# FFN up product by blocks, seven products for eight, on a normalised input, with weight sums added by DMA into the raw tiles

## The chip, the cores and the metric

The kernel runs on one core of one Trainium2 chip. The time is the device time of one execution in microseconds (us); lower is better. The engines are TensorE (PE; its weight loads are listed as PEld), VectorE (DVE), ScalarE (ACT), GpSimd (POOL) and SyncE (SP, which here only issues DMAs). DMA transfers are issued by SP, ACT or POOL and run on 16 shared DMA engines.

## What is computed

One layer of a hybrid encoder block on x of 512 tokens x 1024 channels, all in float32: an RMS norm, a joint input projection, gated linear attention (GLA) and forgetting attention (FoX) side by side, a gated merge, an output projection, and then the FFN that the change is about. Cut to that part:

```python
x = x + y @ w_out                                            # (512, 1024)
a, val = jnp.split(rmsnorm(x, norm_ffn_g) @ w_up, 2, axis=-1)    # w_up: 1024 x 5632
a = causal_dwconv(a, conv_w, conv_b)                         # width 3, over tokens
return rmsnorm(x + (jax.nn.gelu(a) * val) @ w_down, norm_final_g)   # w_down: 2816 x 1024
```

RMS norm divides each token by its root mean square, so the division can be done before or after the product with w_up.

## The kernel before

Features lie on the 128 partitions and tokens on the free axis. D = 1024 channels are KD = 8 blocks of 128; the FFN width of 2816 is NF = 22 feature tiles of 128, for `a` and for `val` each.

**A product in three matmuls.** To keep float32 accuracy, each operand is split into a high part (a cast to float32r) and a low part (what is left). `mm3` multiplies high by high, high by low and low by high: three matmuls, each up to 512 columns wide, with a stationary operand of 128 x 128.

**Weights as pieces.** All weights come through one list of pieces of 128 x 1024 floats (512 KB), numbered in the order of use. A piece is loaded from DRAM into a `raw` tile by SP, cast to `wh` by ScalarE and its residual `wl` is made by VectorE (`split_next`). `piece()` hands out the next piece and first splits up to NW = 3 pieces ahead; `wh` and `wl` have three buffers, `raw` has two (NRAW), and in the down product two more (NRAWX). Pieces 8 to 23 are the token products, 24 to 35 the gates used within the FoX attention, 36 to 51 the other gates and the branches, 52 to 59 w_out, then w_up and w_down.

**Order of the work.** The order in which instructions are written in the code is a priority. A scheduler places them on each engine in that order, but takes a later one when an earlier one isn't ready by its estimate; each engine then runs its own list strictly in order. In the attention, `fill` mixes gate products among the heads by a hand-written pattern, and `load_cb` brings the forget-gate rows `cb` of a head from DRAM (`nct`) one head ahead, with a POOL addition after each.

**From w_out to the FFN.** For each of eight channel blocks, w_out's product gives the new x (`xr`); ScalarE and VectorE make its scaled high and low parts `x2h`, `x2l` (not yet divided by the root mean square), POOL sums squares into `ssum`, and TensorE transposes `xr` into `x2t` for the final residual. The first feature tile of the up product follows; then `rms_of_sum` forms the per-token factor `rb` (ones matmul, a reciprocal root on VectorE, a broadcast by an identity matmul, a copy on ScalarE).

**Up product.** For each f of 22, two `feature_tile` calls (`pa` for `a`, `pv` for `val`) of 8 x 3 matmuls of 512 columns. VectorE multiplies `pa` by `rb` into `ap` with two columns of zeros in front; the convolution is an Identity with scale and bias on ScalarE and two taps on VectorE, then a Gelu on ScalarE, a POOL product with `rb`, and a VectorE product with `pv` into `act`. Meanwhile VectorE forms the sums of activations that the down product needs, and POOL issues eight DMAs that build four sums of blocks of w_down in DRAM (`wsum`).

**Down product.** It is already done by blocks, with seven products of half-size blocks for eight (`product`, p = 0 to 6): 512 columns per matmul, with one piece used up in 12 matmuls. Its last product runs 256 columns at a time for half of the tokens, then the final norm and the stores follow.

Of the kernel before, what the change touches and what calls it, by code (L numbers as in the profile page):

```python
# [18 lines left out]
P = 128  # L19
# [31 lines left out]
NW = 3  # L51


@with_exitstack
def hybrid_kernel(ctx: ExitStack, tc, xT, wp, wd, wf, pp, aw2, qkg, fing, out):
# [21 lines left out]
    def pmm():  # L77
        return bank("mm")
# [12 lines left out]
    down_blocks = [wd[0], wsum[0], wsum[1], wd[2], wsum[2], wd[3], wsum[3]]  # L91
    ND = KD + wp.shape[0]
    NP = ND + NPB * len(down_blocks)

    def width(n):
        return 512 if n >= ND and (n - ND) % NPB == NPB - 1 else 1024

    raws, splits, taken, first_copy = [], [], [0], []
    spare = {}

    def load_raw():
        n = len(raws)
        if n < KD:
            raws.append(slabs[n])
            nc.sync.dma_start(slabs[n], wf[n])
            return
        if n >= ND + NRAW + NRAWX and (n - ND) % (NRAW + NRAWX) >= NRAW:
            raw = xpool.tile([P, 1024], F32, tag="xc", name="raw", bufs=NRAWX)
        else:
            raw = wpool.tile([P, 1024], F32, tag="raw", name="raw", bufs=NRAW)  # L110
        if n < ND:
            nc.sync.dma_start(raw, wp[n - KD])
        else:
            c, m = (n - ND) % NPB * 1024, width(n)
            nc.sync.dma_start(raw[:, :m], down_blocks[(n - ND) // NPB][:, c : c + m])
        raws.append(raw)

    def split_next():
        n = len(splits)
        raw = raws[n]  # L120
# [12 lines left out]
        else:  # L133
            m = width(n)
            nc.scalar.copy(out=hi[:, :m], in_=raw[:, :m])  # L135
            nc.vector.tensor_sub(out=lo[:, :m], in0=raw[:, :m], in1=hi[:, :m].bitcast(F32))  # L136
        splits.append((hi, lo))

    def piece():
        n = taken[0]  # L140
        taken[0] += 1
        while len(splits) < min(NP, n + NW + sum(i in spare for i in range(n + NW))):
            if len(raws) == len(splits):
                load_raw()
            split_next()
            while len(raws) < min(NP, len(splits) + NRAW + (NRAWX if len(raws) >= ND + NRAW else 0)):
                load_raw()
# [62 lines left out]
    cpool.tile([P, 56], F32, name="padc")  # L210
# [43 lines left out]
    def fill(n=1 << 30):  # L254
# [9 lines left out]
    xab = [xpool.tile([P, (KD - NRAWX) * T], F32R, name=f"x{c}") for c in "hl"]  # L264
    xc = [xpool.tile([P, 1024], F32R, tag="xc", name=f"xc{i}", bufs=NRAWX) for i in range(NRAWX)]
    xh, xl = (
        [xab[i][:, k * T : (k + 1) * T] for k in range(KD - NRAWX)] + [c[:, i * T : (i + 1) * T] for c in xc]
# [868 lines left out]
```

## Time and profile before

| | |
|---|---|
| runs, us | 730.02, 730.12, 731.63 (median 730.12) |
| profiled execution, us | 731.21 |
| its span, first to last instruction, us | 729.5 |
| granted TensorE clock | 0.997 |
| DMA moved, MB | 108.78 (mean 149 GB/s) |

The profile is of one execution. Its time is 1.7 us longer than its span and 1.1 us above the median of the runs. Every row names an engine, a line of the code (L136 is line 136), the tile written and the tiles read, shapes and counts; the idle time of an engine before a group and what ended it stand behind the bar. Matmuls are pipelined, so the duration of one is longer than the spacing from one to the next. Lines 151 to 153 are the three matmuls of `mm3`, whatever product calls it; lines 135 and 136 are the cast and the residual of a weight piece.

### The profile page before, as it was taken

The page shows a single profiled execution, that of the slowest core. Times are in us where ns is not written, and L with a number is a line of the kernel's source. Part 1 is how long each engine was busy: PE and PEld are TensorE (multiplying, and loading weights), DVE is VectorE, ACT ScalarE, POOL GpSimd, SP SyncE. Part 2 cuts the span into 40 slices and gives each one's busy share as a digit, 9 for nine tenths or more (in the row PEclk, how much of TensorE's full clock was granted, in tenths as well). Part 3 has the DMA queues.
Part 4 walks back from the last instruction along what each step waited for, and adds up shares of the span by engine and source line. Part 5 has one row for each costly group of instructions (what it writes and reads, how often), then busy time and mean ns, then how long its engine had stood idle before and what let it go on. Part 6 is the DMA issues. An engine that isn't in the chain of part 4 may idle for free.

```text
span 729.5 us, 9416 instructions
## 1 busy us (share of the span) xinstructions
PE 718.7 (99%) x3466; PEld 591.5 (81%) x3466; DVE 473.4 (65%) x751; ACT 351.2 (48%) x578; POOL 154.1 (21%) x162
## 2 busy tenths in 40 slices
PE   8999999999999999999999999999999999999996
PEld 5887788888888888888788888888888888788885
DVE  7774586677766766565435655555636566887876
ACT  6484324588877733234424333323322334555654
POOL 6224234323320301111221111011111011000113
PEclk9999999999999999999999999999999999999998
DMA  8153112324432242333323957788886734476653
GB/s 289 51 149 126 59 61 84 116 97 129 101 134 76 78 139 87 97 106 116 131 87 116 336 193 240 255 209 204 199 224 166 193 117 135 153 217 193 188 183 129
DMA packets 33982, 108.78 MB, mean 149 GB/s; under 512 B 3704, under 2 KB 6920, under 8 KB 33936
## 3 DMA queue, kind: packets, MB, share of 16 engines
q1 hardware_dynamic: 27552, 81.38, 34.7%
q0 software_dynamic: 4224, 23.07, 12.9%
q10 hardware_dynamic: 2160, 3.74, 1.5%
q8 instruction: 27, 0.44, 0.2%
q14 instruction: 19, 0.16, 0.1%
HBM read 106.05 MB, written 25.18 MB: 180 GB/s over the span
## 4 chain that ended last, share of the span: by engine, by line
PE 89%; DVE 3%; issue 3%; DMA 2%; ACT 1%; POOL 1%; ACTq 0%; SPq 0%; DVEq 0%; POOLq 0%
PE ps_mm L151 26%; PE ps_mm L152 25%; PE ps_mm L153 25%; PE ps_ax L152 2%; PE ps_ax L153 2%; PE ps_ax L151 2%; DVE wl L136 1%; PE ps_pt L687 1%; ACT wh L135 1%; DMA raw<-wsum 1%; DMA raw<-in_wd_dram 1%; PE ps_po L711 1%; PE ps_ax L825 1%; DMA qf<-in_wf_dram 1%; PE ps_lg L661 1%
## 5 line engine op out<-in xcount | busy, mean ns | idle before, releaser
L135 ACT CAST wh<-raw 128x1024 fp32r<-128x1024 f32 x134 | 137.7, 1029 | 221.6 <-PE ps_mm L152 116.3
L136 DVE TENSOR_TENSOR wl<-raw,wh 128x1024 fp32r<-128x1024 f32 x134 | 176.4, 1318 | 57.9 <-ACT wh L135 57.3
L151 PE MATMUL ps_mm<-xh,wh 128*128 128x512 f32 x408 | 159.9, 393 | 0.9 <-DVE wh L130 0.9
L153 PE MATMUL ps_mm<-xh,wl 128*128 128x512 f32 x408 | 159.1, 390 | 0.8 <-DVE wl L131 0.8
L152 PE MATMUL ps_mm<-xl,wh 128*128 128x512 f32 x408 | 158.9, 390 | 0.0
L153 PEld LDWEIGHTS ps_mm<-xh,wl 128*128 128x128 f32 x408 | 76.5, 188 | 17.5 <-DVE wl L131 1.4
L151 PEld LDWEIGHTS ps_mm<-xh,wh 128*128 128x128 f32 x408 | 76.6, 188 | 17.1 <-ACT xh L315 1.7
L152 PEld LDWEIGHTS ps_mm<-xl,wh 128*128 128x128 f32 x408 | 76.7, 188 | 15.1
L886 POOL TENSOR_TENSOR t<-t,rb 128x512 f32<-128x512 f32 x22 | 29.3, 1333 | 204.9 <-ACT t L885 204.9
L151 PE MATMUL ps_mm<-wh,xh 128*128 128x512 f32 x162 | 64.0, 396 | 0.0
L152 PE MATMUL ps_mm<-wl,xh 128*128 128x512 f32 x162 | 63.2, 390 | 0.0
L153 PE MATMUL ps_mm<-wh,xl 128*128 128x512 f32 x162 | 63.2, 390 | 0.0
L151 PE MATMUL ps_mm<-xc,wh 128*128 128x512 f32 x136 | 53.2, 391 | 0.0
L152 PE MATMUL ps_mm<-xc,wh 128*128 128x512 f32 x136 | 53.1, 391 | 0.0
L153 PE MATMUL ps_mm<-xc,wl 128*128 128x512 f32 x136 | 53.0, 390 | 0.0
L892 DVE TENSOR_TENSOR act<-ps_mm,t 128x512 f32<-128x512 f32 x22 | 15.2, 692 | 41.3 <-POOL t L886 41.3
L151 PEld LDWEIGHTS ps_mm<-wh,xh 128*128 128x128 f32 x162 | 30.4, 188 | 7.4 <-issue 0.7
L153 PEld LDWEIGHTS ps_mm<-wh,xl 128*128 128x128 f32 x162 | 30.4, 188 | 6.4
L152 PEld LDWEIGHTS ps_mm<-wl,xh 128*128 128x128 f32 x162 | 30.4, 188 | 6.3 <-DVE wl L136 0.2
L413 POOL TENSOR_TENSOR cb<-cb,negm 128x128 f32<-128x128 f32 x32 | 19.2, 606 | 77.0 <-DMA cb<-nct 71.4
L881 DVE SCALAR_TENSOR_TENSOR t<-ap,ppt,t 128x512 f32<-128x512 f32 x44 | 32.7, 749 | 0.7
L968 POOL TENSOR_TENSOR x2t<-x2t,fgt 128x512 f32<-128x512 f32 (+1 forms) x9 | 12.2, 1358 | 93.9 <-ACT t L959 90.4
(316 smaller groups left out, 1299.3 us busy)
## 6 DMA issues: line engine op xcount, KB each, us to landing
raw<-in_wp_dram SPq DMA_DIRECT2D x96, 512.0 KB, 3.3
wsum<-in_wd_dram POOLq DMA_DIRECT2D x6, 2816.0 KB, 14.7
raw<-wsum SPq DMA_DIRECT2D x20, 512.0 KB, 4.0
raw<-in_wd_dram SPq DMA_DIRECT2D x15, 512.0 KB, 3.6
wsum<-wsum POOLq DMA_DIRECT2D x2, 2816.0 KB, 20.9
xr<-in_xT_dram SPq DMA_DIRECT2D x8, 256.0 KB, 4.3
cb<-nct SPq DMA_DIRECT2D x8, 256.0 KB, 6.9
xr<-in_xT_dram ACTq DMA_DIRECT2D x8, 256.0 KB, 3.4
```

Source lines behind the costliest of these rows:

```text
L135: nc.scalar.copy(out=hi[:, :m], in_=raw[:, :m])
L136: nc.vector.tensor_sub(out=lo[:, :m], in0=raw[:, :m], in1=hi[:, :m].bitcast(F32))
L151: mm(ps, lhsT=ah, rhs=bh, start=start, stop=False, **k)
L152: mm(ps, lhsT=ah, rhs=bl, start=False, stop=False, **k)
L153: mm(ps, lhsT=al, rhs=bh, start=False, stop=stop, **k)
L413: nc.gpsimd.tensor_add(out=cb[:, o + n - P : o + n], in0=cb[:, o + n - P : o + n], in1=negm)
L661: mm(lg[:, :n], lhsT=qt0[:, q], rhs=kt[:, :n], start=True, stop=False)
L687: nc.tensor.transpose(pt[:, c], pr[:, c], ident)
L881: nc.vector.scalar_tensor_tensor(out=t0, in0=ap[:, w : w + T], scalar=col(C_CW + w * NF + f), in1=t0, op0=ALU.mult, op1=ALU.add)
L886: scaled = nc.gpsimd.tensor_mul(out=t0, in0=t0, in1=rb)
L892: nc.vector.tensor_mul(out=act[j][:, :, k], in0=pv.rearrange("p (i t) -> p i t", t=H), in1=t0.rearrange("p (i t) -> p i t", t=H))
L968: nc.gpsimd.tensor_mul(out=x3, in0=x3, in1=fgt[:, c])
```

## The change

Two of the 22 features keep the plain form (NCL = 2). For the other 20, taken two at a time (NSS = 10 steps), the up product is done by blocks: the 1024 channels are halved, the 512 tokens are halved, and `a` and `val` are the two halves of the output. Eight block products are replaced by seven (numbers 1 to 7) on sums of blocks of x and of w_up, Winograd's form of Strassen's method.

- The sums need one x for all, so x is normalised first: `xs`, kept as float32, is multiplied by `rb` on VectorE; four sums and seven operands' high and low parts follow (`split_x`, `minus_sum`). The POOL product with `rb` after the Gelu goes, except for the two plain features.
- A product uses one piece in 24 matmuls of 256 columns (`up_product`). The order of the products of neighbouring steps is interleaved by `SLOT`: 2, 3, 6, the next step's 1, 7, the next step's 5, 4.
- The weights' sums are not stored. A raw tile is loaded with a block, and another block is added to it by a DMA that POOL issues with an add: product 5 is loaded and added to at once; products 6, 4 and 7 add to the tile of 5, 6 and 3 after that has been split (`recipes`, `follows`). Four loads and four adds of 512 KB are made per step.
- The results are combined in PSUM and on VectorE and ScalarE: product 6 adds onto product 1's result through a sum `u`, copied back into its bank, onto which 7 and then 4 accumulate.
- The eight DMAs for the sums of w_down move from the up product to the splits of pieces 24, 27, 30, 33, 38, 42, 46 and 50, each behind a small POOL copy (`tick`).
- The transposed x goes to DRAM (`x2d`) by way of a tile `st`, and is read back by a POOL DMA after the up product. `s1` and `s2` take the places of activations no longer needed.
- The plain pairs run side by side over k, and `rms_of_sum` runs inside the first of them.

The diff, cut to its core:

```diff
+SLOT = {1: -3, 5: -1, 2: 1, 3: 2, 6: 3, 7: 5, 4: 7}
+SUM_AT = (24, 27, 30, 33, 38, 42, 46, 50)
...
+    steps = sorted((7 * g + at, g, p) for g in range(NSS) for p, at in SLOT.items())
...
+        new, before, place = {
+            1: ((u11,), None, "raw"), 2: ((u21,), None, "raw"), 3: ((u22,), None, "raw"), 5: ((u12, u11), None, "rawx"),
+            6: ((u22,), 5, "rawx"), 4: ((u21,), 6, "rawx"), 7: ((u12,), 3, "raw"),
+        }[p]
...
+    def load_raw(n):
+        new, before, m, place = recipes[n]
+        if before is not None:
+            raws[n] = raws[before]
+            return
...
+        nc.sync.dma_start(raws[n][:, :m], new[0])
+        for w in new[1:]:
+            nc.gpsimd.dma_start(raws[n][:, :m], w, accum_op=ALU.add)
+
+    def load_ahead(n):
+
+        for i in range(n, min(NP, n + 6)):
+            new, before, _, place = recipes[i]
+            if place == "rawx":
+                ahead = 6 if rawx_pool and i < ND else NRAW + NRAWX if rawx_pool else 0
+            else:
+                ahead = NRAW if i < ND - 7 * NSS else 3 if i < ND else NRAW + NRAWX
+            if i not in raws and i < n + ahead and (before is None or before in raws):
+                load_raw(i)
...
         splits.append((hi, lo))
+        if n in follows:
+            nc.gpsimd.dma_start(raw, recipes[follows[n]][0][0], accum_op=ALU.add)
+        if n in sums_at:
+            i, b, op = sums_at[n]
+            now = nc.gpsimd.tensor_copy(out=tick, in_=lo[:, 0:1].bitcast(F32))
+            with tc.issue_after(now.ins):
+                nc.gpsimd.dma_start(wsum[i], b, accum_op=op, max_dma_last_dim=KB * 512)
...
-        nc.any.tensor_copy(
-            out=x2t[:, :, c * P : (c + 1) * P], in_=pt.rearrange("p (t c) -> p t c", c=P)
-        )
+        st = bpool.tile([P, NT, P], F32, tag="st", name="st", bufs=2)
+        nc.scalar.copy(out=st, in_=pt.rearrange("p (t c) -> p t c", c=P))
+        nc.scalar.dma_start(x2d[:, :, c * P : (c + 1) * P], st)
+        nc.scalar.activation(out=xs[:, c], in_=xr, func=AF.Copy, scale=col(C_FFN + c))
...
+    plain.append((pmm(), pmm()))
+    up = (piece(), piece())
+    plain_products(plain[0], up, range(2))
+    rms_of_sum(ssum, rt, rb, cpool, "r1", between=lambda: plain_products(plain[0], up, range(2, 6)))
+    plain_products(plain[0], up, range(6, KD))
...
+    def split_x(p, src):
+        nc.scalar.copy(out=xops[p][0], in_=src)
+        nc.vector.tensor_sub(out=xops[p][1], in0=src, in1=xops[p][0].bitcast(F32))
+
+    def minus_sum(out, a, b):
+        nc.vector.scalar_tensor_tensor(out=out, in0=a, scalar=-1.0, in1=b, op0=ALU.mult, op1=ALU.subtract)
+
+    for k in range(KD):
+        nc.vector.tensor_mul(out=xs[:, k], in0=xs[:, k], in1=rb)
+    split_x(1, x11)
+    nc.vector.tensor_sub(out=x3, in0=x11, in1=x21)
+    nc.vector.tensor_sub(out=x21, in0=x22, in1=x21)
+    split_x(5, x21)
+    plain.append((pmm(), pmm()))
+    up = (piece(), piece())
+    plain_products(plain[1], up, range(KD))
+    split_x(2, x12)
+    minus_sum(x11, x21, x11)
+    minus_sum(x12, x12, x11)
+    split_x(3, x12)
+    split_x(6, x11)
+    split_x(7, x3)
+    split_x(4, x22)
...
+    def up_product(ps, p, first):
+
+        wh, wl = piece()
+        ah, al = xops[p]
+        for i in range(2):
+            for k in range(KH):
+                c = slice((i * KH + k) * P, (i * KH + k + 1) * P)
+
+                mm3(
+                    ps[:, i * H : (i + 1) * H], wh[:, c], wl[:, c], ah[:, k], al[:, k], first and i == k == 0,
+                    k == KH - 1, skip_group_check=True,
+                )
...
+    for g, p in steps:
...
+        up_product(ps, p, first)
+        if p == 1 or p == 5:
+            st[p] = joint()
+            nc.scalar.copy(out=st[p], in_=ps)
+        elif p == 6:
+            u = joint()
+            nc.vector.tensor_add(out=u, in0=ps, in1=st[1])
+            nc.scalar.copy(out=ps, in_=u)
+            minus_sum(ap[:, :, 2 : H + 2], halves(st["z"]), halves(u))
+        elif p == 7:
+            minus_sum(ap[:, :, H + 2 : T + 2], halves(ps), halves(st[5]))
+            t0 = st["t0"] = npool.tile([P, 2, T], F32, tag="t0", name="t0")
+            for i in range(2):
+                convolve(f + i, i, t0)
+        elif p == 4:
...
+                    nc.vector.tensor_mul(
+                        out=act[j][:, i, k], in0=halves(c)[:, fs], in1=t0[:, fs, i * H : (i + 1) * H]
+                    )
+            for j, k, _ in parts:
+                sums_of_acts(j, k)
...
+    nc.gpsimd.dma_start(x2t, x2d)
+    nc.gpsimd.dma_start(fgt, fing.broadcast_to([P, D]))
```

207 lines of the change are left out of this document (119 added, 88 removed).

## The prediction

> **What bounds the kernel now.** I read the page's busy table and chain first, then TensorE in order of time around the FFN up product, then stage windows, DMA and groups by line.
>
> ```profile
> PE 718.7 (99%) x3466; PEld 591.5 (81%) x3466; DVE 473.4 (65%) x751; ACT 351.2 (48%) x578; POOL 154.1 (21%) x162
> ...
> PE 89%; DVE 3%; issue 3%; DMA 2%; ACT 1%; POOL 1%; ACTq 0%; SPq 0%; DVEq 0%; POOLq 0%
> ```
>
> TensorE is busy 99% of the span and carries 89% of the chain. A matmul less is worth its spacing, as long as what feeds it keeps pace. TensorE in order of time gives two spacings; the second comes from the last product, whose tail is computed 256 columns at a time.
>
> ```profile
> 374.27 0.39 PE L151 MATMUL ps_mm<-xh,wh 128*128 128x512 f32 x1
> ...
> 596.34 0.39 PE L151 MATMUL ps_mm<-xh,wh 128*128 128x512 f32 x1
> ...
> 616.74 0.39 PE L151 MATMUL ps_mm<-wh,acth 128*128 128x512 f32 x1
> ...
> 717.00 0.28 PE L153 MATMUL ps_ax<-wh,actl 128*128 128x256 f32 x1
> ...
> 723.00 0.28 PE L152 MATMUL ps_mm<-ws,acth 128*128 128x256 f32 x1
> ```
>
> The up product runs from 374.27 to 616.74, 242.5 us. Its last 90 spacings (596.34 to 616.74) are 0.2267 us each; 50 spacings at 256 columns (717.00 to 723.00) are 0.1200 us. The 0.39 and 0.28 are pipelined durations. Half the columns cost 53% of the time. 44 tiles x 24 = 1056 matmuls x 0.2267 = 239.4 us fill the stage, so it has almost no idle time to win; only fewer columns can win.
>
> Stage windows (columns: stretch; its length and the busy us and count of PE, PEld, DVE, ACT, POOL; clock; DMA share; GB/s):
>
> ```profile
> 640.00:700.00 60.00, 60.00 (x266) 49.68 (x265) 49.75 (x64) 36.21 (x54) 6.10 (x4) 1.00 0.66 199
> 327.00:376.00 49.00, 49.00 (x230) 39.21 (x229) 23.69 (x26) 21.37 (x32) 12.96 (x8) 1.00 0.34 116
> 172.00:176.00 4.00, 3.37 (x18) 2.63 (x16) 3.89 (x10) 3.51 (x8) 2.84 (x5) 1.00 0.39 139
> ```
>
> The down product (first row) already uses up one weight piece per 12 matmuls, 2.72 us, with VectorE at 83% and TensorE never idle. That is the nearest precedent for the changed up product. The third row, in the attention, is a place where TensorE does fall idle.
>
> **The change, part by part.** Matmuls first. Two features keep the plain form (96 matmuls). The other 20 become ten steps of seven products, each 24 matmuls of 256 columns: 1680 x 0.1200 = 201.6 us in place of 960 x 0.2267 = 217.6 us: **-16.0 us**. One eighth of the columns would be 27 us; the rest is lost to the dearer short matmul. The Trainium skill, TensorE: Matmul & The Clock Gate, section Back-to-back issue gap, gives N/2.4 GHz plus about 2.5 ns for an isolated gap, 109 and 216 ns; by it the estimate would be 1680 x 0.109 - 960 x 0.216 = -24 us. The rows above read 120 and 226.7 ns, so the trace disagrees with the page and decides.
>
> A product now uses up a 512 KB piece in 24 x 0.1200 = 2.88 us where a piece lasted 24 x 0.2267 = 5.44 us. So VectorE and ScalarE must be costed. Groups by line within the up product (busy, mean ns):
>
> ```profile
> L136 DVE TENSOR_TENSOR wl<-raw,wh 128x1024 fp32r<-128x1024 f32 x37 | 45.2, 1222 | 32.2 <-ACT wh L135 32.1
> L881 DVE SCALAR_TENSOR_TENSOR t<-ap,ppt,t 128x512 f32<-128x512 f32 x36 | 27.0, 749 | 0.6
> L892 DVE TENSOR_TENSOR act<-ps_mm,t 128x512 f32<-128x512 f32 x20 | 13.8, 692 | 38.0 <-POOL t L886 38.0
> L875 DVE TENSOR_TENSOR ap<-ps_mm,rb 128x512 f32<-128x512 f32 x18 | 12.4, 687 | 10.2 <-PE ps_mm L153 10.2
> L135 ACT CAST wh<-raw 128x1024 fp32r<-128x1024 f32 x37 | 38.8, 1049 | 83.4 <-DMA raw<-in_wp_dram 48.9 <-PE ps_mm L152 34.5
> L877 ACT ACTIVATE t<-ap,ppt 128x512 f32<-128x512 f32 x18 | 14.7, 816 | 8.9 <-DVE ap L875 8.9
> L885 ACT ACTIVATE t<-t 128x512 f32<-128x512 f32 x18 | 11.4, 632 | 34.1 <-DVE t L881 34.1
> L886 POOL TENSOR_TENSOR t<-t,rb 128x512 f32<-128x512 f32 x20 | 25.8, 1292 | 184.6 <-ACT t L885 184.6
> ```
>
> Steady state, per step of 7 x 2.88 = 20.2 us. VectorE: 7 weight residuals x 1.22 = 8.5; the sum u and two differences, 0.69 + 2 x 0.75; four conv taps, 3.0; two gate products, 1.4; sums of activations 1.4 (first half) or 2.2: 16.5 to 17.3 us, 82 to 86%. ScalarE: 7 casts 7.3, three copies and one split at about 0.6 (0.57 at L826, below), two Identity 1.6, two Gelu 1.3: 12.6 us, 62%. That is the down product's load (83%, 60%), so TensorE stays the bound. One loop can still bite: product 6 ends, VectorE adds u (0.69), ScalarE copies u back into the bank (about 0.6), product 7 accumulates on it; only the next step's product 1 (2.88 us) lies between. The loop takes 1.5 us with both engines free and 3.6 with a residual (1.22) and a cast (1.05) ahead of it, so it costs 0 to 0.7 us a step. I take **+1 us** in all; the upper end is a rival. The POOL product by rb goes for these 20 features; it only delayed VectorE, so that is worth nothing.
>
> The start of the stage. Rows in order of time:
>
> ```profile
> 376.34 0.57 ACT L826 COPY x2t<-ps_ax 128x512 f32<-128x512 f32 x1
> 376.58 1.78 POOL L822 TENSOR_TENSOR ssum<-ssum,sq 128x512 f32<-128x512 f32 x1 [4.24 <-ACT sq L821]
> 385.01 1.05 ACT L135 CAST wh<-raw 128x1024 fp32r<-128x1024 f32 x1 [8.10 <-PE ps_mm L152]
> 385.72 0.95 PE L241 MATMUL ps_ax<-ones,ssum 128*128 128x2 f32 x8
> 385.76 0.34 ACTq L909 DMA_DIRECT2D fgt<-in_fing_dram  x1
> 388.28 0.16 DVE L186 TENSOR_SCALAR r1w<-r1v 128x4 int32<-128x4 int32 x1
> 388.35 1.22 DVE L136 TENSOR_TENSOR wl<-raw,wh 128x1024 fp32r<-128x1024 f32 x1
> 389.49 0.16 DVE L189 TENSOR_SCALAR rt<-r1w 128x4 int32<-128x4 int32 x1
> 391.56 1.13 PE L246 MATMUL ps_ax<-ident,rt 128*128 128x128 f32 x8 [0.42 <-DVE rt L195]
> ```
>
> The norm now runs inside the first plain pair: ssum is there at 376.58 + 1.78 = 378.4; 36 matmuls of the pair (8.2 us from 374.27) with the ones product and four transposes end at about 383.7; the broadcast (1.13) and a copy (0.6) follow, so rb stands at about 385.4. That removes the 0.42 us idle (**-0.4**). The second pair now needs both its pieces at once, and the second piece's buffer comes free only when the first pair ends (the 8.10 us wait at 385.01); cast and residual, 2.3 us, against 0.7 us of matmuls and 0.45 more that do without the residual: **+0.8 us** (0 to 1.2).
>
> Then the dear part. From rb to the end of product 6 of the first step TensorE has 2.0 (rest of pair one) + 10.9 + 5 x 2.88 = 27.3 us of work. VectorE has, before that point in code order: 8 normalising products 5.5, four sums and seven operand residuals 11 x 1.22 = 13.4, six weight residuals 7.3, both conv epilogues 7.1: 33.3 us. What can wait (two operand residuals, one sum and split) is 3.8, so the wait is at least 33.3 - 3.8 - 27.3 = 2.2 us. If VectorE keeps strictly to code order, product 2's weight residual ends 30.9 us after rb, while TensorE gets there after 18.7: 12.2 us. The row at 388.35, a weight residual set inside the reciprocal-root chain, shows that gaps are filled out of order, so I take the middle, **+7 us**.
>
> DMA. The DMA view for 400 to 600 us (queues: packets, MB, share of 16 engines; issues: KB, us to landing), and last the queue row of 522 to 543.5, one add:
>
> ```profile
> q0 software_dynamic: 4224, 23.07, 47.0%
> q1 hardware_dynamic: 5253, 19.16, 27.3%
> ...
> raw<-in_wp_dram SPq DMA_DIRECT2D x36, 512.0 KB, 6.2
> wsum<-in_wd_dram POOLq DMA_DIRECT2D x6, 2816.0 KB, 14.7
> wsum<-wsum POOLq DMA_DIRECT2D x2, 2816.0 KB, 20.9
> ```
> ```profile
> q0 software_dynamic: 528, 2.88, 68.9%
> ```
> ```profile
> 522.13 1.02 POOL L890 DMA_DIRECT2D wsum<-wsum  x1
> ```
> ```profile
> raw<-in_wp_dram SPq DMA_DIRECT2D x96, 512.0 KB, 3.3
> ```
>
> A 512 KB load takes 0.273 x 200 / 36.6 = 1.5 us of all engines, an add of that size 0.689 x 21.5 x 512/2816 = 2.7. A step has four of each: 16.8 of 20.2 us, share 0.83. No add into SBUF is in the trace; it lands in 3.3 - 1.5 + 2.7 = 4.5 us on quiet engines and 6.2 - 1.5 + 2.7 = 7.4 on loaded ones. The tightest is product 7's, added to product 3's tile: between the residual of 3 and TensorE's need lie about 11 us, less issue on POOL (1.0), cast and residual (2.3): 7.7 us. Both estimates fit, so 0; beyond 7.7 each us costs ten. Behind a late add stand, on ScalarE, the cast's followers (joint copies, conv scale); on POOL, product 5's add waits for its SP load with the adds for 7 and 4 queued behind it, due later; on SP a load waits for its tile, with at most two behind it.
>
> The four-block sums of w_down move from the up product into the attention and gates, each with a small POOL copy and a 2.8 MB transfer past POOL's and SP's queues there.
>
> ```profile
> 126.30 1.05 ACT L135 CAST wh<-raw 128x1024 fp32r<-128x1024 f32 x1 [4.33 <-PE ps_mm L153]
> ...
> 198.18 1.05 ACT L135 CAST wh<-raw 128x1024 fp32r<-128x1024 f32 x1
> ```
> ```profile
> 174.36 3.38 DMA cb<-nct
> ```
> ```profile
> cb<-nct SPq DMA_DIRECT2D x6, 256.0 KB, 6.9
> ```
>
> The first four (copies, 14.7 us each in the rows above) follow the splits of pieces 24, 27, 30 and 33, whose casts, ten from the first row to the second, are at 126.3 to 198.2 us. The cb load is on the chain where TensorE fell idle (172 to 176), so copies will meet such loads; a cb load comes a head (11 us) ahead, so a delay of 3 to 6 us mostly fits: **+1 us** (0 to 4). The detour of x2 through DRAM adds a ScalarE activation (0.6) and a DMA issue (0.34) per w_out tile (24 x 0.2267 and transposes, 6.0 us), where ScalarE is at 44% (327 to 376): 0, or 7 if that cover were gone. Its reload, 2.5 MB beside the first down pieces, has 16 us: 0 (to 2).
>
> Sum: -16.0 + 1 - 0.4 + 0.8 + 7 + 1 = -6.6. The profiled execution took 731.2, giving 724.6; it lies 1.1 above the median 730.12, which would give 723.5. I say **724**.
>
> **Rivals.** *The hand-over hides.* VectorE's order falls well, only 2.2 us are lost and no loop or cb wait appears: -16.0 - 0.4 + 2.2 = -14.2: 716. For it: gaps are filled out of order; against: 33 us of work in a 27 us window.
>
> *The u loop binds.* The schedule repeats, so a bad phase costs the same each step: 0.7 us x 10 plus followers' slips, about +9 over the forecast: 733. For it: VectorE at 86%; against: the down product at 83% without idle.
>
> *The adds come late (slower).* One mechanism: product 7's add lands after 9.5 us instead of 7.7, because engines at 0.83 queue and POOL's issue (1.0 us) is held by VectorE. Price 10 x 1.8 = +18: 742; it decides against the change from about 8.4 us on. The Trainium skill, SBUF — State Buffer, section Who interferes with whom, says that DMAs issued by GpSimd can be starved of descriptor time by VectorE while those of other queues cannot; no row here isolates that.
>
> *It doesn't do what it says.* Seven products at more than 0.126 us per matmul save less than 6 us; the tail ran 50 in a row at 0.120, so this has 0.05.
>
> **Numbers.** Forecast (720 to 729) 0.42, hidden 0.15, loop 0.20, late adds 0.18, dearer matmuls 0.05. This kernel's measurement can tell about 0.3%, 2.2 us. Faster: 0.39 + 0.15 + 0.02 = 0.56; within: 0.03 + 0.08 + 0.02 + 0.01 = 0.14; slower 0.30. The range 715 to 742 leaves out half of the late adds and a little of the hidden case; the forecast's own is 720 to 729.
>
> **What would show it.** 256-column matmuls at 0.120; VectorE at 82 to 86% in the steps; a TensorE gap of about 7 us before the first step's product 2; adds landing in 4.5 to 7.4 us. ScalarE waiting on DMA in every step, or a gap before each product 7, would make me wrong.

## The result, and the profile after

The changed kernel is slower. Four runs of it gave 739.1, 741.11, 743.35 and 743.6 us (median 742.23), beside 730.54 us for the kernel before on the same chip: a ratio of 1.0152 (95% interval 1.0114 to 1.019). The forecast was 724, with 742 as the end of its range. One of the four executions without adds (a kernel below) took 868.62 us at a granted clock of 0.753, where the other three had 0.994 to 0.995, and it is left out of the medians.

The profiled execution took 743.6 us (span 741.8), 12.3 us of span more than before. It is the longest of the four; between the medians lie 11.7 us. The page of the changed kernel: the busy times, the chain by engine, and the DMA issues (count, KB, median us from issue to landing).

```profile
PE 714.4 (96%) x4186; PEld 620.2 (84%) x4186; DVE 518.7 (70%) x787; ACT 407.4 (55%) x648; POOL 166.9 (23%) x190
...
PE 61%; DMA 17%; DVE 9%; issue 6%; ACT 4%; POOL 1%; SPq 0%; ACTq 0%; POOLq 0%; DVEq 0%
...
wsum<-in_wd_dram POOLq DMA_DIRECT2D x6, 2816.0 KB, 18.4
raw<-in_wu_dram SPq DMA_DIRECT2D x30, 512.0 KB, 4.5
rawx<-in_wu_dram POOLq DMA_DIRECT2D x30, 512.0 KB, 5.8
...
raw<-in_wu_dram POOLq DMA_DIRECT2D x10, 512.0 KB, 7.2
```

TensorE's share of the chain fell from 89% to 61%, and 17% of it is now DMA, which had 2%. The last row is product 7's add: 7.2 us at the median.

Where the 12.3 us went can be read from TensorE in order of time: the first matmul of the up product, the first and the last of 48 at 256 columns in a step, and the last of product 4 in the last step.

```profile
378.96 0.39 PE L200 MATMUL ps_mm<-xh,wh 128*128 128x512 f32 x1
...
457.88 0.28 PE L200 MATMUL ps_ax<-xh,wh 128*128 128x256 f32 x1
...
463.52 0.28 PE L202 MATMUL ps_ax<-xh,wl 128*128 128x256 f32 x1
...
630.00 0.28 PE L202 MATMUL ps_mm<-xc,wl 128*128 128x256 f32 x1
```

- Up to the up product: it begins at 378.96 where it began at 374.27: +4.7. (In the profiles of the kernels below that do the same work up to there it begins between 375.5 and 378.8, so this execution stands at the late end.)
- The up product ends at 630.1. Six matmuls of the down product stand inside it (1.4 us), so it took 249.8 us, where it took 242.5: +7.3. Two products run from 457.88 to 463.52, 47 spacings of 0.120 us, as forecast, and 16.0 us were saved; so 23.3 us of new idle and slow time stand in this stage.
- From there to the end: 113.1 against 112.8: +0.3. The three add up to 12.3.

If each start on TensorE is compared with the start before it plus the plain spacing of that matmul's shape, the changed kernel loses 9.8 us in the hand-over (376 to 440 us), 9.8 in the steps (440 to 615) and 5.6 at the end (615 to 640). The kernel before loses 1.9 in the same way around its norm, so 7.9 of the hand-over are new, and the three make up the 23.3. A typical stall of the steps, in rows of POOL, of ScalarE, of VectorE and of TensorE in order of time; the last fence is one piece of the chain in the same stretch (start, us, what):

```profile
458.58 0.86 POOL L149 DMA_DIRECT2D rawx<-in_wu_dram  x1 [7.61 <-DVE wl L181]
459.12 1.21 POOL L184 DMA_DIRECT2D raw<-in_wu_dram  x1
461.14 0.86 POOL L184 DMA_DIRECT2D rawx<-in_wu_dram  x1 [0.82 <-DVE wl L181]
```
```profile
468.00 1.05 ACT L180 CAST wh<-raw 128x1024 fp32r<-128x1024 f32 x1 [6.05 <-DMA raw<-in_wu_dram]
...
470.94 0.59 ACT L1031 COPY ps_ax<-joint 128x512 f32<-128x512 f32 x1 [0.95 <-DVE joint L1030]
```
```profile
469.08 1.23 DVE L181 TENSOR_TENSOR wl<-raw,wh 128x1024 fp32r<-128x1024 f32 x1 [5.88 <-ACT wh L180]
470.22 0.69 DVE L1030 TENSOR_TENSOR joint<-ps_ax,joint 128x512 f32<-128x512 f32 x1
```
```profile
471.58 0.39 PE L200 MATMUL ps_ax<-xh,wh 128*128 128x256 f32 x1 [2.02 <-ACT ps_ax L1031]
```
```profile
459.12 8.78 DMA raw<-in_wu_dram
```

POOL issues three adds within 2.6 us: product 5's (458.58), product 7's (459.12), product 4's (461.14). Product 7's lands after 8.78 us, and product 5's, ahead of it, after 5.39. ScalarE stands 6.05 us at its cast; behind the cast come VectorE's low part, only then u (L1030) and its copy (L1031), and product 7 starts 2.02 us late. From the cast's start to that of product 7 it is 3.58 us. Product 7 was due at 471.58 - 2.02 = 469.56, so the cast had to start at 465.98: the add had 6.9 us to land.

Windows of the changed kernel (columns as in the prediction: stretch; its length and the busy us and count of PE, PEld, DVE, ACT, POOL; clock; DMA share; GB/s):

```profile
413.42:417.80 4.38, 4.32 (x19) 3.92 (x20) 4.12 (x6) 4.12 (x6) 0.00 (x0) 0.61 0.41 120
...
440.00:590.00 150.00, 145.26 (x1180) 144.44 (x1179) 108.98 (x134) 82.23 (x102) 24.16 (x28) 0.98 0.84 196
...
471.58:475.90 4.32, 4.32 (x23) 4.32 (x24) 2.41 (x3) 1.53 (x2) 0.86 (x1) 0.60 0.61 143
```

The count in the middle row is the measure used below: 150 us hold 1250 matmuls at 0.120, and here they held 1180. The first and last rows are stretches right after a stall: the granted clock is 0.61 and 0.60 (0.50 from 472.60 to 475.80, where matmuls start 0.213 us apart instead of 0.120), and a stall of 2 to 3 us costs about 1.5 us more.

### The profile page after: what moved, and what is told of

Same layout as the page of the kernel before. It is cut to its first block, busy times and chain, and to the rows that moved or that the text cites. A ratio compares the mean times of both kernels' runs of the same rounds, so it can differ in the third digit from the quotient of the medians.

```text
span 741.8 us, 11096 instructions
## 1 busy us (share of the span) xinstructions
PE 714.4 (96%) x4186; PEld 620.2 (84%) x4186; DVE 518.7 (70%) x787; ACT 407.4 (55%) x648; POOL 166.9 (23%) x190
## 4 chain that ended last, share of the span: by engine, by line
PE 61%; DMA 17%; DVE 9%; issue 6%; ACT 4%; POOL 1%; SPq 0%; ACTq 0%; POOLq 0%; DVEq 0%
PE ps_mm L200 15%; PE ps_mm L201 14%; PE ps_mm L202 14%; DMA rawx<-in_wu_dram 7%; DMA raw<-in_wu_dram 6%; DVE wl L181 4%; PE ps_ax L201 4%; PE ps_ax L200 4%; PE ps_ax L202 4%; ACT wh L180 3%; DMA raw<-in_wp_dram 2%; DVE t L970 1%; DMA cb<-nct 1%; DMA rawx<-wsum 1%; PE ps_pt L737 1%
## 5 line engine op out<-in xcount | busy, mean ns | idle before, releaser
L200 PE MATMUL ps_mm<-xh,wh 128*128 128x512 f32 (+1 forms) x288 | 102.0, 355 | 4.1 <-ACT ps_mm L1031 3.3
L202 PE MATMUL ps_mm<-xh,wl 128*128 128x512 f32 (+1 forms) x288 | 100.8, 351 | 0.0
L201 PE MATMUL ps_mm<-xl,wh 128*128 128x512 f32 (+1 forms) x288 | 100.8, 351 | 0.0
L181 DVE TENSOR_TENSOR wl<-rawx,wh 128x1024 fp32r<-128x1024 f32 (+1 forms) x48 | 57.8, 1208 | 7.3 <-ACT wh L180 7.0
L180 ACT CAST wh<-rawx 128x1024 fp32r<-128x1024 f32 (+1 forms) x48 | 49.1, 1023 | 16.5 <-DMA rawx<-in_wu_dram 9.1
L200 PE MATMUL ps_ax<-xh,wh 128*128 128x256 f32 x120 | 35.8, 299 | 5.1 <-ACT ps_ax L1031 5.1
L200 PE MATMUL ps_ax<-xo,wh 128*128 128x256 f32 x120 | 34.2, 285 | 3.1 <-ACT wh L180 3.1
L202 PE MATMUL ps_ax<-xh,wl 128*128 128x256 f32 x120 | 35.4, 297 | 0.1
L201 PE MATMUL ps_ax<-xl,wh 128*128 128x256 f32 x120 | 35.2, 293 | 0.0
L201 PE MATMUL ps_ax<-xo,wh 128*128 128x256 f32 x120 | 34.1, 284 | 0.0
L202 PE MATMUL ps_ax<-xo,wl 128*128 128x256 f32 x120 | 34.0, 283 | 0.0
```

What stands on the lines that cost most here:

```text
L200: mm(ps, lhsT=ah, rhs=bh, start=start, stop=False, **k)
L201: mm(ps, lhsT=ah, rhs=bl, start=False, stop=False, **k)
L202: mm(ps, lhsT=al, rhs=bh, start=False, stop=stop, **k)
```

## The experiments

Each group of runs had the kernel before beside it (median 730.5 to 731.3 us); the ratios are to those runs.

| kernel | median us | ratio to before, 95% interval |
|---|---|---|
| changed kernel | 742.23 | 1.0152 (1.0114 to 1.019) |
| no adds | 725.14 | 0.9916 (0.9895 to 0.9936) |
| no sums of w_down | 739.74 | 1.0113 (1.0094 to 1.0133) |
| neither | 722.27 | 0.9881 (0.9865 to 0.9897) |
| no add for product 5 | 731.34 | 1.0011 (0.9995 to 1.0026) |
| no add for product 4 | 741.18 | 1.0147 (1.0088 to 1.0205) |
| adds of 5 and 7 swapped | 746.03 | 1.0195 (1.0164 to 1.0226) |
| u ahead of product 7's split | 741.29 | 1.0141 (1.0126 to 1.0156) |
| before, with the sums moved alone | 734.17 | 1.0041 (1.0026 to 1.0056) |
| product 7 later | 732.5 | 1.002 (1.0003 to 1.0038) |
| three edits | 743.51 | 1.0178 (1.0149 to 1.0207) |
| three edits, sums earlier | 749.89 | 1.0259 (1.019 to 1.0328) |
| product 7 later, hand-over | 731.63 | 1.0015 (1.0 to 1.003) |
| product 7 later, last step | 725.88 | 0.9927 (0.9903 to 0.995) |
| both | 725.37 | 0.9915 (0.9884 to 0.9947) |
| both, u early | 724.05 | 0.9893 (0.9876 to 0.9909) |

The theory after the result: the adds into the raw tiles come late, and the moved sums cost something too. Its first rival: the loop of product 6, u and product 7 is too long by itself, for TensorE's releaser in the rows is u's copy, not a DMA.

**No adds.**

```diff
-        for w in new[1:]:
-            nc.gpsimd.dma_start(raws[n][:, :m], w, accum_op=ALU.add)
...
-        if n in follows:
-            nc.gpsimd.dma_start(raw, recipes[follows[n]][0][0], accum_op=ALU.add)
```

> Left out: all 40 DMAs that add one weight block into a raw tile; the products read the first block alone, so every matmul, cast, subtraction and the whole steady loop stay, only these DMAs and their waits go. Theory A (the adds come late): in a step the add for product 7 lands 8.6 to 8.8 us after its issue, ScalarE's cast of that tile waits about 6 us for it, and behind the cast and VectorE's low part stand u and its copy, for which product 7 waits; the same thing happens once before product 6 in the hand-over and once at the end of the up part. Without adds the TensorE idle between 376 and 640 us falls from 24 to 5 to 9 us (what is left is the ones' matmul, 0.8, and the queue of the plain epilogue, 2 to 4), half-clock stretches there go too, and the time is 724 to 728. Rival B (the loop product 6, u, product 7 is too long by itself, or VectorE is too full): the stalls of about 2 us ahead of product 7 stay in the same steps, and the time stays at 738 to 742. The idle of attention, 100 to 376 us, stays at 10 us by both.

725.14 us, as the theory said. Its window of the steps:

```profile
440.00:590.00 150.00, 150.00 (x1252) 150.00 (x1251) 115.62 (x140) 85.69 (x107) 0.00 (x0) 1.00 0.36 106
```

The steps run at the full pace of 1250, with every cast, residual and u still in them. So the loop is not too long by itself, and the adds cost about 17 us. What stayed was the hand-over, where only 1.8 us less were lost; its longest wait is now for VectorE's backlog:

```profile
414.33 0.58 PE L198 MATMUL ps_ax<-xh,wl 128*128 128x256 f32 x1 [2.33 <-DVE wl L179]
```

**No sums, and neither.** Left out are the eight DMAs of w_down's sums.

```diff
-    down_blocks = [b11, wsum[0], wsum[1], b21, wsum[2], b22, wsum[3]]
+    down_blocks = [b11, b12, b22, b21, b22, b22, b21]
...
-        if n in sums_at:
-            i, b, op = sums_at[n]
-            now = nc.gpsimd.tensor_copy(out=tick, in_=lo[:, 0:1].bitcast(F32))
-            with tc.issue_after(now.ins):
-                nc.gpsimd.dma_start(wsum[i], b, accum_op=op, max_dma_last_dim=KB * 512)
```

> Left out: the eight DMAs that form the sums of w_down in DRAM, with the one-column copies on POOL that time them; the down part reads plain blocks of w_down instead. Theory C (the move of the sums into attention costs): TensorE's idle of 100 to 376 us falls from 10.5 to about 4.3, which is what the kernel before had there, and the time from 742 to 735 to 737; the idle of 376 to 640 stays near 24. Rival (the same idle comes from the x2 detour or from the new order of the loads): 740 to 742.

> Left out: both the 40 adds into raw tiles and the eight sums. If adds and sums have separate costs in separate places, theories A and C together, the idle is that of the kernel before plus the hand-over's 3 to 6 us, and the time is 718 to 722. If one cost only gives way to another (the steps wait for something else as soon as the adds are gone), 730 or more.

739.74 and 722.27 us; 735 to 737 was expected of the first, and 722 was the end of the range of the second. The idle of attention, gates and w_out went as expected, and the up product began 5.7 us earlier (at 373.28), but the time fell by only 2.5, because the adds' stalls fell at other steps and were larger there. Where no adds disturb, leaving out the sums gave 2.9 us (725.14 to 722.27). So costs of adds and sums lie in separate places, and the sums' is 2.5 to 2.9 us.

**The kernel before, with the sums moved alone.** The same lines, in the kernel before:

```diff
-    sum_steps = {2 * i: (i, b, ALU.bypass) for i, b in enumerate((b12, b22, b22, b21))}
-    sum_steps.update({8: (0, b11, ALU.add), 10: (2, b12, ALU.add), 12: (1, wsum[0], ALU.add), 15: (3, wsum[1], ALU.add)})
...
+        if n in sums_at:
+            i, b, op = sums_at[n]
+            now = nc.gpsimd.tensor_copy(out=tick, in_=lo[:, 0:1].bitcast(F32))
+            with tc.issue_after(now.ins):
+                nc.gpsimd.dma_start(wsum[i], b, accum_op=op, max_dma_last_dim=KB * 512)
```

> Nothing left out. The kernel before with one part of the change alone: the eight DMAs that form the sums of w_down, moved from the up part to splits 24 to 50, in attention, the gates and w_out. The prediction gave this +1 us, 0 to 4; leaving the sums out of the changed kernel gave 2.5 and 3.7 us back. If their cost is that of their place, the time is 733 to 735 with 3 to 6 us more idle on TensorE between 100 and 376 us and none elsewhere; if the place is free and only the adds' neighbourhood made them cost, 729 to 731.

734.17 us: +3.3 (the 3.7 in the expectation is the 2.9 above). The stretch 240 to 340 us (gates and w_out), first in the kernel before, then with the sums moved:

```profile
240.00:340.00 100.00, 100.00 (x446) 82.49 (x445) 65.25 (x65) 38.89 (x51) 16.87 (x13) 1.00 0.33 106
```
```profile
240.00:340.00 100.00, 98.52 (x432) 80.22 (x432) 56.58 (x63) 37.07 (x50) 22.89 (x21) 1.00 0.86 213
```

The sums raise the DMA share there from 0.33 to 0.86, and 432 matmuls stand where 446 stood: 14 x 0.2267 = 3.2 us, the whole cost. Before, the same DMAs ran inside the up product without idle.

**One add fewer: product 5's, or product 4's.** The same traffic is cut at two places of POOL's queue.

```diff
# no add for product 5
-        for w in new[1:]:
-            nc.gpsimd.dma_start(raws[n][:, :m], w, accum_op=ALU.add)
# no add for product 4
-        if n in follows:
+        if n in follows and recipes[n][1] is None:
```

> Order of the changed kernel. Left out: only the add into product 5's tile (10 DMAs of 40), which in a stalled step is issued about half a microsecond ahead of product 7's add in the same POOL queue; all else stays. If product 7's add is late because another add stands right ahead of it, its median landing falls from 7.2 us towards the 4.5 to 5 of a lone load, the casts no longer wait, and of the 9 to 10 us of TensorE idle in the steps (440 to 615 us) 3 or less stay: 731 to 735. If it is late because the DMA engines are loaded as a whole (82 to 90% busy), a quarter less adding gives a part of that, the same as the next kernel: 735 to 739.

> The other half of the pair. Left out: only the add into product 4's tile (10 DMAs of 40), which is issued about 2 us after product 7's add. The traffic cut is the same as in the kernel without product 5's add. If the place in the queue decides, product 7's add still takes 7 us and more and the idle of the steps stays at 6 to 10 us: 738 to 742. If the load as a whole decides, the same as the other: 735 to 739.

731.34 and 741.18 us. Product 7's add, first without product 5's ahead of it, then without product 4's behind it:

```profile
raw<-in_wu_dram POOLq DMA_DIRECT2D x10, 512.0 KB, 5.6
```
```profile
raw<-in_wu_dram POOLq DMA_DIRECT2D x10, 512.0 KB, 7.5
```

The DMA load as a whole is not what delays it: a quarter less adding behind it changes nothing that can be measured, and the same quarter ahead of it is worth 10.9 us. In the steps of the changed kernel no cast waited for product 5's own add, so the gain is not that wait. ScalarE still waits 2.3 to 2.5 us at product 7's cast in every step without product 5's add, and TensorE hardly notices: that much the window allows. An add takes 0.552 x 190 / 35 = 3.0 us of all engines (share of POOL's queue and the 26 + 9 adds, 425 to 615 us, in the DMA view):

```profile
q0 software_dynamic: 5051, 18.40, 55.2%
...
rawx<-in_wu_dram POOLq DMA_DIRECT2D x26, 512.0 KB, 5.8
...
raw<-in_wu_dram POOLq DMA_DIRECT2D x9, 512.0 KB, 7.6
```

Two adds issued 0.54 us apart follow one another: in the step shown the second lands 3.9 us behind the first (467.90 and 463.97). Over the eight steps in which all three are issued, product 5's add lands after 5.3 to 6.9 us, product 7's after 6.2 to 8.8 and product 4's, the third, after 7.3 to 10.6.

**The two adds swapped.**

```diff
         for w in new[1:]:
-            nc.gpsimd.dma_start(raws[n][:, :m], w, accum_op=ALU.add)
+            if n < at_step[1, 5]:
+                nc.gpsimd.dma_start(raws[n][:, :m], w, accum_op=ALU.add)
+            else:
+                held.append((n, m, w))
...
-            nc.gpsimd.dma_start(raw, recipes[follows[n]][0][0], accum_op=ALU.add)
+            seven = nc.gpsimd.dma_start(raw, recipes[follows[n]][0][0], accum_op=ALU.add)
+            if recipes[n][1] is None and recipes[n][3] == "raw":
+                while held:
+                    k, km, w = held.pop()
+                    with tc.issue_after(seven.ins):
+                        nc.gpsimd.dma_start(raws[k][:, :km], w, accum_op=ALU.add)
```

> Nothing left out, order of the products as in the changed kernel. From the second step on, the add into product 5's tile is held in POOL's queue until product 7's add has been issued; nothing else changes. If the place in the queue is the whole cause of the stalls in the steps, product 7's add lands in 5.5 to 6 us as it did without product 5's add, product 5's add lands late instead but is needed one product (2.88 us) later, and the time falls to 730 to 735 with the same DMA traffic. If product 5 now waits in product 7's stead, the stalls stay, ahead of another product: 738 to 743. (An earlier expectation put two products at 11.6 us; they are 5.8.)

746.03 us: the rival's case, and worse than it. Product 7's add now lands in 5.6 us, and the lateness has passed to product 5 (rows of ScalarE):

```profile
466.54 1.05 ACT L184 CAST wh<-raw 128x1024 fp32r<-128x1024 f32 x1 [3.14 <-DMA raw<-in_wu_dram]
471.84 1.04 ACT L184 CAST wh<-rawx 128x1024 fp32r<-128x1024 f32 x1 [4.25 <-DMA rawx<-in_wu_dram]
472.79 0.58 ACT L1040 COPY ps_ax<-joint 128x512 f32<-128x512 f32 x1
```

Product 5's add, issued 0.54 us behind, took 10.23 us. ScalarE waits 4.25 us at product 5's cast, and u's copy for product 7, which product 5's add has nothing to do with, stands behind it.

**u ahead of product 7's split.** If the cost were only that u stands behind the waiting cast, this edit would cure it.

```diff
-        wh, wl = piece()
+        wh, wl = piece(1 if p == 6 else 0)      # one split fewer ahead
...
-            nc.vector.tensor_add(out=u, in0=ps, in1=st[1])
-            nc.scalar.copy(out=ps, in_=u)
+            u_sum = nc.vector.tensor_add(out=u, in0=ps, in1=st[1])
+            u_copy = nc.scalar.copy(out=ps, in_=u)
+            with tc.issue_after(u_sum.ins), tc.issue_after(u_copy.ins):
+                split_next()
+            load_ahead(len(splits))
```

> Nothing left out, order of the products and of the adds as in the changed kernel. Alone changed: the split of product 7 (ScalarE's cast, VectorE's low part) is queued behind u and u's copy, where u's sum and copy stood behind that split and so behind its wait for the add. If the cost of a late add is that u waits in the queues behind the cast (head of line), the stalls ahead of product 7 in the steps and of the first step fall from about 2 us to 0.3 to 1 each, most half-clock stretches go with them, and the time is 731 to 736 with the adds as late as before. If product 7 itself waits for its block (add, cast, low part, 8.8 + 1.05 + 1.22 us) the stalls keep their size: 738 to 743.

741.29 us: the theory of the queue fell. u's copy is out of the way and product 7 waits for its own cast instead (a row of TensorE):

```profile
491.77 0.39 PE L200 MATMUL ps_mm<-xh,wh 128*128 128x256 f32 x1 [1.76 <-ACT wh L180]
```

So u's copy was only the last link that showed. The late block costs by itself. (Product 7's add also landed later here, 8.0 us at the median and 10.26 in the step shown, so the run doesn't tell what u first would be worth with the adds at 7.2.)

**Product 7 later.** It changes places with the next step's product 5 (the order is 2, 3, 6, next 1, next 5, 7, 4).

```diff
-SLOT = {1: -3, 5: -1, 2: 1, 3: 2, 6: 3, 7: 5, 4: 7}
+SLOT = {1: -3, 5: -2, 2: 1, 3: 2, 6: 3, 7: 6, 4: 7}
```

> Nothing left out. In each step product 7 and the next step's product 5 change places: 2, 3, 6, next 5, 7, next 1, 4 in place of 2, 3, 6, next 1, 7, next 5, 4 is NOT what is made; the order becomes 2, 3, 6, next 1, next 5, 7, 4, so that between product 6 and product 7 lie two products (11.6 us) and not one, and the add for product 7 has one product more to land. Theory A: the stalls ahead of product 7 go (7 to 9 us of idle with their half-clock stretches), the rest stays: 732 to 735. If instead the add comes late however much time it has, because the queue of adds itself is full (60% of the DMA engines' time in 425 to 615 us), the stalls move to product 4 or to product 5 and the time stays within 738 to 742.

732.5 us, 9.7 less. (Two products are 5.8 us; the 11.6 was a slip.) Product 7's add now lands in 7.7 us at the median, no faster than before, and the steps keep their pace:

```profile
440.00:590.00 150.00, 149.97 (x1246) 149.57 (x1245) 117.61 (x143) 85.00 (x108) 25.20 (x30) 1.00 0.91 211
```

The DMA engines are busier than in the changed kernel (0.91 against 0.84), mostly because more of the work falls into the same 150 us (1246 matmuls against 1180). Time for the add was what lacked.

**Three edits, and the sums earlier.** The order above, with products 2 and 3 exchanged in every step, and the hand-over rearranged; then the sums moved as well.

```diff
-SLOT = {1: -3, 5: -2, 2: 1, 3: 2, 6: 3, 7: 6, 4: 7}
+SLOT = {1: -3, 5: -2, 3: 1, 2: 2, 6: 3, 7: 6, 4: 7}
...
-    split_x(7, x3)                    # now behind product 2 of the first step
-    split_x(4, x22)                   # now behind product 6
...
# plain epilogues: behind products 3 and 2 of the first step
# sums earlier
-SUM_AT = (24, 27, 30, 33, 38, 42, 46, 50)
+SUM_AT = (15, 17, 19, 22, 27, 31, 35, 39)
```

> Nothing left out. Product 7 after the next step's product 5, as in the kernel that took 732.5 us; products 2 and 3 change places, so that product 7's add, which starts behind the split of product 3, has one product more again (this matters in the last step, where no next products stand between); and in the hand-over the splits of x for products 7 and 4 and the epilogues of the plain products stand behind products 3, 2 and 6 in the program and not ahead of product 1. By the theory of the backlog, the hand-over's 3.4 us ahead of product 6 and its half-clock 2.2 go, and the end's 4.3 with half-clock 1.9 go but for about 1: 721 to 726, faster than the kernel before. If the hand-over's wait only moves to a later product (to u of the first step, or to product 4 for its split), 728 to 731.

> Nothing left out. The kernel with the three edits, and the eight sums of w_down at splits 15, 17, 19, 22, 27, 31, 35, 39 (63 to 252 us) in place of 24 to 50 (130 to 311 us): into 60 to 140 us, where the DMA engines were 20 to 28% busy without sums. If the sums cost by what they do to the raw loads of the gates and w_out between 220 and 340 us, the idle of 100 to 376 us falls from 7 to 10 us to 4.5 to 6 and the time by 2 to 4 us against the kernel with three edits: 718 to 723. If they cost by POOL's extra copies and queue wherever they stand, or if the early part has no slack either, the same or 1 to 3 us slower.

743.51 and 749.89 us; both expectations missed. By the order of the tiles, with 2 behind 3 the tile for the next step's product 1 comes free one product later, and its plain load is late: the longest such wait, where that load was issued at 582.47 and took 9.39 us beside the adds (ScalarE, then TensorE, in the kernel with three edits):

```profile
591.95 1.05 ACT L180 CAST wh<-raw 128x1024 fp32r<-128x1024 f32 x1 [6.20 <-DMA raw<-in_wu_dram]
```
```profile
593.05 0.39 PE L200 MATMUL ps_mm<-xo,wh 128*128 128x256 f32 x1 [3.17 <-ACT wh L180]
```

The earlier sums met the attention instead of the gates: a single wait of TensorE there was 2.87 us, where the kernel with three edits had none of over 1 us.

```profile
178.04 0.55 PE L760 MATMUL ps_po<-ph,v 128*128 128x256 f32 x1 [2.87 <-ACT ph L744]
```

**Hand-over and last step, one by one.** Both from the kernel with product 7 later.

```diff
# hand-over: epilogues and splits of x for 7 and 4 later, as above, and
+        if (g, p) == (0, 6):
+            with tc.issue_after(last_mm.ins):
+                last_mm = up_product(ps, p, first)
# last step: order 3, 6, 2, 7, 4
+    slot_last = {**SLOT, 3: 1, 6: 2, 2: 3}
```

> Nothing left out. The order that took 732.5 us (product 7 after the next step's product 5), with the hand-over alone edited: the splits of x for products 7 and 4 and the epilogues of the plain products stand later, and product 6's matmuls of the first step are kept behind product 3's, where the order on TensorE had two of them standing ahead of 46 of products 2 and 3. If that order and VectorE's queue are what the hand-over's 3.4 us and the half-clock 2.2 behind it come from, they go: 726 to 730. If u of the first step, or product 4's split, only waits in its place: 731 to 734.

> Nothing left out. The order that took 732.5 us, with the last step alone in the order 3, 6, 2, 7, 4: product 7's add then has three products (8.6 us) and not two (5.8 us) between the split of 3 and its own, and product 4's the same. If the stall at the end of the up part (4.3 us and 1.9 at half clock) comes from the last add of product 7 having less time than it needs, 727 to 730. If it comes from the matmuls of the down part set ahead of product 7, or from ScalarE's queue, 731 to 733.

> Nothing left out. Both of the edits before this one, hand-over and last step. If they lie in separate places and neither wait only moves, their gains add up: 721 to 726, faster than the kernel before by 0.7 to 1.3%. If not, 728 or more.

The last step's order gave 725.88 us, 6.6 less and faster than the kernel before, a little more than expected: in the last step no next products stand between 6 and 7, so its add had had the least time of all. The edit gives product 4's add one product more as well. In the kernel with three edits, where only product 7's had it, ScalarE waited 2.34 us for product 4's add (617.41) and a stall of 3.41 us stayed, so product 7's add is not the whole of the end. The stretch that holds the end, before (product 7 later) and with the edit:

```profile
590.00:640.00 50.00, 46.63 (x274) 41.42 (x274) 41.45 (x56) 29.06 (x40) 2.82 (x4) 0.93 0.69 204
```
```profile
590.00:640.00 50.00, 50.00 (x307) 45.05 (x307) 47.20 (x63) 31.99 (x45) 2.82 (x4) 1.00 0.79 244
```

The hand-over's edit gave nothing that can be measured (731.63, and 725.37 with the other, inside the range expected of both, but by the last step alone). The wait of 3.2 us ahead of product 6 went, one of 0.9 came ahead of another product, and one of 2.95 us came ahead of the first product 7:

```profile
426.78 0.58 PE L202 MATMUL ps_ax<-xh,wh 128*128 128x256 f32 x1 [2.95 <-ACT ps_ax L1045]
```

**u early.** In the kernel with both, the end of the plain epilogue, the split of x for 4 and the first sums of activations stand behind u.

```diff
+        if (g, p) == (1, 1):
+            for i, (_, pv) in enumerate(plain):
+                nc.vector.tensor_mul(out=act[0][:, :, i], in0=halves(pv), in1=halves(t0p[:, i]))
+            split_x(4, x22)
+            sums_of_acts(0, slice(0, NCL))
```

> Nothing left out. The kernel with both edits (725.4 us), and in the hand-over the last part of the plain epilogue, the split of x for product 4 and the first sums of the activations stand behind u of the first step. If the 3.1 us ahead of product 7 in the first step and the 2.4 us at half clock behind it come from u standing behind these on VectorE and ScalarE, they fall to under 1: 720 to 723. If another wait takes the place again: 724 to 726.

724.05 us, the fastest kernel that leaves nothing out: 1.1% faster than the kernel before. Against the 725.37 without this edit the intervals overlap, and the profile, which is of the slowest of its five runs (728.41), shows that the wait moved once more (3.47 us, to a cast, at 429.31). What bounds the hand-over at last, whether VectorE's work in it or the order on several queues, stays open.

## Why the prediction was wrong, step by step

- **Matmuls, -16.0: right.** 0.120 us held in every step that was not stalled or at the low clock.
- **Adds, 0: the step that failed.** "Both estimates fit, so 0; beyond 7.7 each us costs ten." Three things in it were wrong. The landing was estimated for one add on evenly loaded engines (up to 7.4), and the median, 7.2, even agrees. But the adds come in a burst of three, and the second of them took 8.78; the order on POOL was written down in the prediction ("product 5's add waits for its SP load with the adds for 7 and 4 queued behind it") and not priced. The need was 6.9, not 7.7, since u and its copy stand behind the cast. And in the last step no next step's product gives time: there the add landed in 5.42 us, with none right ahead of it, and its cast still waited 2.55 us (615.04). Steps and end together lost about 15.4 us where +1 was put; leaving out the adds gave 17 back, 1.8 of it in the hand-over.
- **The rival "the adds come late"** had 0.18 and 742, and that is the time that came. That product 7's add lands too late is what the runs show. That the number agrees so well is in part luck: it said 18 for ten equal stalls and only the forecast's own terms beside; the runs give about 17 for all adds, with unequal stalls, and the rest from the sums and the hand-over. The cause it gave, "engines at 0.83 queue and POOL's issue (1.0 us) is held by VectorE", isn't the one, as far as the load as a whole goes: a quarter less load behind the add left its landing at 7.5 us, the same quarter ahead of it brought 5.6, and the issues in the rows took 0.86 and 1.21 us.
- **The rival "the u loop binds"** looked right in the rows, where u's copy releases TensorE. Without adds u costs nothing, and with u first in the queues the stalls stay. (Its loop is 0.69 + 0.6 = 1.3 us by the prediction's own terms, not 1.5; the rows from 470.22 to 471.53 say the same.)
- **VectorE at 82 to 86%** was too high: 78% at full pace (117.61 of 150 us with product 7 later).
- **Moved sums, +1 (0 to 4): mis-sized.** Measured alone 3.3. The four early ones were looked at beside the loads of `cb`; what was lost came mostly between 240 and 340 us, where the prediction looked at no row for the sums.
- **Hand-over, +7 with +0.8 and -0.4: right in size** (7.9, of it about 1.6 at the low clock), in part by luck. Of its price only the part of the backlog was foreseen; product 6's add (cast waiting 2.48 us at 412.32) and product 7's were in it too. The gap, 3.1 us and not 7, stood ahead of product 6's first two matmuls, which the scheduler had put ahead of product 2's.
- **The low clock after a stall: not in the sum.** Four stretches of about 1.5 us each in the up product, 6.2 of the 23.3 and part of the terms above; a fifth stood in w_out.

Forecast -6.6, measured +12.3 in the profiled execution: 18.9 apart. Of these the steps are 8.8, the end 5.6, the time up to the up product 3.7 (the moved sums, and the late start of this execution), the hand-over 0.5 and the down part 0.3, each read to a few tenths.

The Trainium skill, SBUF — State Buffer, section Who interferes with whom, was quoted in the prediction for descriptors of GpSimd's DMAs that VectorE starves. The runs explain the lateness by the adds ahead in the queue and do not need it; none isolates it.

## What to carry to other kernels

A transfer that follows a use of the same buffer has a fixed window. Count that window in the order actually issued, with the transfers that stand right ahead of it in the same queue, and compare it with the landing of the second or third in a burst, not with an average. Here the remedy was more products between the use and the need, for the adds and for every other transfer whose tile the new order moves; and when TensorE's releaser is a short copy, look at what the copy's engine waited for just before.

## What the runs showed of the hardware that was not expected

**The low clock comes after short stalls.** In the changed kernel a wait of 2.02 us (471.58) was followed by the window at 0.60 above, and one of 1.96 us (428.98) was not. In the profiles of the study every stall of 2.8 us or more was followed by it, single stalls under 1.5 us were not, and between these both occur. Two waits close together can do it too: the stretch in w_out came behind 0.70 us (333.32) and 0.84 us (334.67). The Trainium skill, TensorE: Matmul & The Clock Gate, section What's actually happening, puts half rate after an idle window of about 3.4 us, which is free-running. The rows are shorter than that; the measured waits decide. Each such stretch lasted 3 to 6 us.

**VectorE beside POOL.** A weight residual that takes 1.22 us took 3.75 while POOL ran two products of 512 columns (VectorE, then POOL):

```profile
418.48 1.22 DVE L181 TENSOR_TENSOR wl<-rawx,wh 128x1024 fp32r<-128x1024 f32 x1
419.86 3.75 DVE L181 TENSOR_TENSOR wl<-raw,wh 128x1024 fp32r<-128x1024 f32 x1 [0.16 <-ACT wh L180]
```
```profile
419.66 2.87 POOL L994 TENSOR_TENSOR t<-t,rb 128x512 f32<-128x512 f32 x2
```

The Trainium skill, SBUF — State Buffer, section Who interferes with whom, says that a VectorE instruction with two SBUF inputs contends with a GpSimd instruction that reads SBUF; the trace agrees.
